# Cross-attention output projection as seven block products, and the first two up slices in one loop

## The chip, the core and the metric

The program runs on one core of a Trainium2 chip. The core has five engines with an instruction queue each: TensorE (PE, with PEld for its weight loads), VectorE (DVE), ScalarE (ACT), GpSimd (POOL) and SyncE (SP). The metric is the device time of one execution in microseconds (us). Before the change the median of three runs is 857.94 us (857.85 to 858.04). The profile is one more execution, of 858.13 us.

## The reference

One layer of an encoder on 512 tokens of width 1024, in float32: a token mixer with recurrent heads, a cross-attention to 256 memory tokens, and a squared-ReLU MLP, each added to the residual stream x, and a norm at the end. What matters here:

```python
def cross_attention(xn, memn, w_q, w_kv, w_o):
    q = (xn @ w_q).reshape(b, s, XATTN_HEADS, XATTN_HEAD_DIM)      # 4 heads of 256
    k, v = jnp.split(memn @ w_kv, 2, axis=-1)
    ...
    p = jax.nn.softmax(scores, axis=-1).astype(v.dtype)
    o = jnp.einsum('bhqk,bkhd->bqhd', p, v).reshape(b, s, D_MODEL)
    return o @ w_o                                                 # 512x1024 @ 1024x1024

x = x + cross_attention(rmsnorm(x, norm_xattn), rmsnorm(mem, norm_mem), w_q, w_kv, w_o)
x = x + jnp.square(jax.nn.relu(rmsnorm(x, norm_mlp) @ w_up)) @ w_down
```

## The kernel before, in words

**Number format.** Every projection is done in three passes of TensorE: an operand is split into a high part (a rounded copy, ACT, L232) and a low part (the rest, DVE, L233), and high x high, high x low and low x high are accumulated in one PSUM bank (`mm3`, L236 to L238). A weight block of 128x1024 is loaded by SP into one of three `st` buffers (L211) and split into one of three `wh`/`wl` pairs.

**Cross-attention.** The loop over the four heads (L904) projects q with `proj_d`, and puts a chain (`xattn_chain`) in a list. `tick()` takes the next step of the oldest chains, so that a head's scores, transposes and product with v (PV) are issued among the matmuls of the projection that follows. A head's output is os_[2h] and os_[2h+1], both transposed (features on the partitions, 512 tokens along them).

**Output projection.** `proj_res("xo", ...)` (L914) computes x + o @ w_o in eight pieces of 128 tokens by 512 columns (`xr[t, c]`, tiles named `vv`). For each column half c it takes four weight blocks of 256 rows, one for each head, and accumulates 4 token tiles x 8 feature tiles x 3 passes = 96 matmuls of 128x512; both halves take 192. The argument `drain` finishes all chains ahead of the fourth head's block. A finished piece is added to the residual (L823), its squares are summed (`stats`, ACT, L817), and `transp` turns it on TensorE (L831) and writes the high and low part of the MLP's input, `x3T[c]`, with four ACT and four DVE instructions (L836, L837). x3T[0] holds features 0 to 511, x3T[1] the rest.

**MLP.** The 4096 hidden features go in four blocks f. Each has eight up slices (`proj_d`, 24 matmuls each), and then the down projection of the block, which is already done in seven products instead of eight, in the manner of Strassen and Winograd (P1 to P7, L1048 to L1095). Tokens, features and columns are halved; the products take sums of weight blocks, "T2", "U" and "T3". POOL makes these sums by DMA: it loads a block into an `as` buffer (two of 128x2560) or a `gate` buffer (two of 128x1024), waits until it has landed, and issues the next block as an accumulating DMA on top (`sum_loads`, `add_block`, L937 to L952). The number g (0 or 1) is the half of a block's features that one weight tile holds. For f = 0 the sums are issued ahead of the first up slice.

**Order.** Up to the MLP a scheduler sets the order of the instructions on each engine; then TensorE keeps the order of the code (L1006). Each engine takes its instructions strictly in that order.

Of the kernel before, what the change touches and what calls it, by code (L numbers as in the profile page):

```python
# [11 lines left out]
F32R = mybir.dt.float32r  # L12
# [33 lines left out]
def _split_order():  # L46
    def d(m, c0, n):
        return [("d", m, 0, c0 + P * i) for i in range(n)]

    def t(m, k0, c0, n=4):  # L50
        return [("t", m, k0 + 2 * i, c0) for i in range(n)]

    seq = t("in", 0, 1536) + [("d", "gate", 0, 0)]
    for g in (0, 512, 1024, 2048):
        seq += d("in", g, 2)
    for g in (0, 512, 1024):
        seq += d("in", g + 256, 2)
# [12 lines left out]
    seq += [("t", "down", 8 * f + 2 * g, 512) for f in range(4) for g in range(2)]  # L70
    return seq


SEQ = _split_order()
SIDX = {key: i for i, key in enumerate(SEQ)}
NSTREAM = len(SEQ) - 8


@with_exitstack
def trunk(ctx: ExitStack, tc: tile.TileContext, x, mem, wpk, vec, cst, lmask, rmask, rows, out):  # L80
# [21 lines left out]
    def tiny(w):  # L102
        return sb.tile([P, w], F32, tag=f"tiny{w}", name=nm("tiny"), bufs=2 if w == 8 else 6)
# [809 lines left out]
    x3T = XT()
    proj_res("xo", 0, os_, (x3T, V_MLP), st2, drain)  # L914
    x3 = xk(x3T)
    ms2 = rstd_tok(st2)
    r4 = tiny(4)
    gp.tensor_tensor(out=r4, in0=ms2, in1=nh.to_broadcast([P, 4]), op=ALU.pow)
    rrow = RG()

    def rms_row():
        ps = smb()
        for t in range(4):
            pe.transpose(ps[:, t * P:t * P + P], r4[:, t:t + 1].to_broadcast([P, P]), ident)
        sc.activation(rrow[:, 0:512], ps, AF.Copy)

    ORDER = ("P1", "P2", "P6", "P5", "P7", "P3", "P4")  # L930
    JOBS = [("P1", 0), ("P2", 0), ("P1", 1), ("P2", 1)] + [(p, g) for p in ORDER[2:] for g in range(2)]
    jobs_hl, sums = {}, {}

    def block(f, g, kh, c):
        return SIDX["t", "down", 8 * f + 2 * g + 4 * kh, 512 * c]

    def sum_loads(f, names):  # L937

        parts = {"T2": ((0, 1), (1, 1), (0, 0)), "U": ((0, 1), (0, 0)), "T3": ((0, 1), (1, 1))}
        for nme in names:  # L940
            t = A16() if nme != "T3" else None
            for g in range(2):
                sums[f, nme, g] = G4()[:, :] if t is None else t[:, g * 1024:g * 1024 + 1024]
        for i in range(3):
            for nme in names:
                for g in range(2):
                    if i < len(parts[nme]):
                        add_block(sums[f, nme, g], block(f, g, *parts[nme][i]), i > 0)
# [40 lines left out]
    def add_to(t, c, ps, sign, fin=False):  # L989
# [13 lines left out]
        gp.tensor_tensor(out=r, in0=s1, in1=nh, op=ALU.pow)  # L1003
        finish(t, r, pieces[t])

    ctx.enter_context(tc.manual_schedule(engines={mybir.EngineType.PE}))  # L1006
    for f in range(4):

        sta = []
        sum_loads(f, ("T2", "U", "T3") if f == 0 else ("T2",))  # L1010
        for p in range(4):
            a = []
            for j in range(2):
                ps, = proj_d("up", 1024 * f + P * (p + 4 * j), x3, count=1)
                if f == 0 and p == 0 and j == 0:
                    rms_row()
# [31 lines left out]
        X, Y, Z = [smb(), smb()], [mmb(), mmb()], [smb(), smb()]  # L1048
        bank = {"P1": X, "P2": Y, "P5": Z, "P6": X, "P3": Z, "P7": X, "P4": X}
        into = {"P1": (0, 0, 1), "P2": (0, 0, 1), "P5": (2, 1, 1), "P6": (0, 1, -1), "P3": (0, 1, 1), "P7": (2, 1, -1), "P4": (2, 0, 1)}  # L1050
        last = {"P2", "P3", "P7", "P4"}

        def product(p, g, u, w, first, end):
            for k in range(2):
                ah, al = [t[:, u * P:u * P + P] for t in sta[2 * g + k][p]]
                bh, bl = [t[:, k * 512:k * 512 + 512] for t in w]
                new = first and k == 0 and p in ("P1", "P2", "P5")
                fl = dict(skip_group_check=True)
                ps = bank[p][u]
                pe.matmul(ps, lhsT=ah, rhs=bh, start=new, stop=False, **fl)  # L1060
                pe.matmul(ps, lhsT=ah, rhs=bl, start=False, stop=False, **fl)  # L1061
                pe.matmul(ps, lhsT=al, rhs=bh, start=False, stop=end and k == 1, **fl)  # L1062

        def ahead(n):
            with tc.high_priority():
                for m in range(n, n + 3):
                    job(f, m)
                i = max(hl_tiles)
                for m in range(i + 1, i + 4):
                    load(m)  # L1070
            if n == 8 and f < 3:
                sum_loads(f + 1, ("U", "T3"))
            return job(f, n)

        def done(p, u):
            t0, c, sign = into[p]
            add_to(t0 + u, c, bank[p][u], sign, fin and p in last)

        n = 0
        while n < len(JOBS):  # L1080
            p, g = JOBS[n]
            if p == "P4":
                ws = [ahead(n), ahead(n + 1)]
                for u in range(2):
                    for g in range(2):
                        product(p, g, u, ws[g], False, g == 1)
                    done(p, u)
                n += 2
                continue
            w = ahead(n)  # L1090
            for u in range(2):
                product(p, g, u, w, g == 0, g == 1)
                if g == 1:
                    done(p, u)
            n += 1  # L1095


# [88 lines left out]
```

## Time and profile before

| | |
|---|---|
| median of three runs | 857.94 us |
| profiled execution, its span | 858.13 us, 856.4 us |
| PE busy | 839.4 us, 98% of the span |
| DVE busy | 567.2 us, 66% |
| ACT busy | 423.9 us, 50% |
| POOL busy | 67.6 us, 8% |
| bytes moved | 113.62 MB, mean 133 GB/s |
| granted TensorE clock | 0.997 of full speed |

The span runs from the first to the last recorded instruction; the execution's own time is 1.7 us longer. A matmul row has its start and a length that includes the draining of the array; since matmuls overlap, what one costs is the distance between the starts of two. Of a wait, the row names the instruction that was waited for. The attention's fourth head and the output projection lie between 455 and 520 us.

### The profile page before, as it was taken

What the parts mean: (1) busy time and instruction counts of PE and PEld (TensorE: products, weight loads), DVE (VectorE), ACT (ScalarE), POOL (GpSimd) and SP (SyncE); (2) the same over time, 40 slices, a digit from 0 to 9 for tenths busy, and PEclk for the clock granted to TensorE, in tenths of its full rate; (3) what the DMA queues carried; (4) which work ended last, traced back from release to release, by engine and by line L of the source; (5) the groups of instructions that cost most, each with busy time, mean ns of one, the idle gap of its engine ahead of it and who ended that gap; (6) DMA issues with size and microseconds to landing.
All of it is one profiled execution on the core that took longest, in us unless ns stands there. A gap on an engine that the chain in (4) does not pass through costs nothing.

```text
span 856.4 us, 11676 instructions
## 1 busy us (share of the span) xinstructions
PE 839.4 (98%) x4438; PEld 692.3 (81%) x4438; DVE 567.2 (66%) x996; ACT 423.9 (50%) x773; POOL 67.6 (8%) x114
## 2 busy tenths in 40 slices
PE   7999999999999999999999999999999999999995
PEld 5888788887977987887888887888888888888884
DVE  5558875599368977555555446677567656756675
ACT  5336454444578485454444346453454344434544
POOL 2000000100010000100001200003101210220001
PEclk9999999999999999999999999999999999999998
DMA  7332224122142332532214842359935982698322
GB/s 266 128 116 77 72 77 137 41 99 81 71 127 74 110 130 91 183 104 98 75 50 130 201 136 96 92 127 237 276 108 143 275 246 99 179 288 196 123 51 98
DMA packets 32682, 113.62 MB, mean 133 GB/s; under 512 B 3761, under 2 KB 3889, under 8 KB 32626
## 3 DMA queue, kind: packets, MB, share of 16 engines
q1 hardware_dynamic: 23120, 78.84, 26.8%
q0 software_dynamic: 9216, 33.56, 17.7%
q8 instruction: 35, 0.57, 0.3%
q10 hardware_dynamic: 290, 0.47, 0.2%
q14 instruction: 21, 0.17, 0.1%
HBM read 110.76 MB, written 2.10 MB: 132 GB/s over the span
## 4 chain that ended last, share of the span: by engine, by line
PE 89%; issue 5%; DVE 2%; ACT 1%; DMA 1%; POOL 1%; POOLq 0%; SPq 0%; ACTq 0%; DVEq 0%
PE mm L236 20%; PE mm L237 20%; PE mm L238 19%; PE sm L1060 5%; PE sm L1061 5%; PE sm L1062 5%; PE sm L384 2%; PE sm L688 2%; PE sm L673 2%; PE sm L454 2%; PE mm L1061 1%; PE mm L1062 1%; PE mm L1060 1%; PE sm L238 1%; PE sm L237 1%
## 5 line engine op out<-in xcount | busy, mean ns | idle before, releaser
L232 ACT ACTIVATE wh<-st 128x1024 fp32r<-128x1024 f32 x133 | 141.0, 1060 | 216.3 <-PE mm L237 114.5
L233 DVE TENSOR_TENSOR wl<-st,wh 128x1024 fp32r<-128x1024 f32 x133 | 162.8, 1224 | 107.1 <-ACT wh L232 106.2
L236 PE MATMUL mm<-xT,wh 128*128 128x512 f32 x544 | 215.9, 398 | 0.0
L237 PE MATMUL mm<-xT,wh 128*128 128x512 f32 x544 | 213.3, 392 | 0.3 <-DVE xT L837 0.3
L238 PE MATMUL mm<-xT,wl 128*128 128x512 f32 x544 | 212.6, 391 | 0.0
L237 PEld LDWEIGHTS mm<-xT,wh 128*128 128x128 f32 x544 | 102.2, 188 | 22.9 <-DVE xT L837 2.0
L236 PEld LDWEIGHTS mm<-xT,wh 128*128 128x128 f32 x544 | 102.2, 188 | 21.9 <-issue 0.7
L238 PEld LDWEIGHTS mm<-xT,wl 128*128 128x128 f32 x544 | 102.1, 188 | 21.3 <-issue 0.2
L952 POOL DMA_DIRECT2D as<-in_wpk x48 | 36.7, 773 | 311.2 <-DVE wl L233 186.6
L1018 DVE SCALAR_TENSOR_TENSOR t<-mm,rg 128x512 f32<-128x512 f32 x32 | 22.1, 692 | 55.2 <-PE mm L238 55.0
L236 PE MATMUL mm<-wh,yT 128*128 128x512 f32 x128 | 50.6, 395 | 0.1
L238 PE MATMUL mm<-wh,yT 128*128 128x512 f32 x128 | 50.4, 394 | 0.0
L237 PE MATMUL mm<-wl,yT 128*128 128x512 f32 x128 | 50.3, 393 | 0.0
L1060 PE MATMUL sm<-wh,yT 128*128 128x512 f32 x128 | 49.8, 389 | 0.0
L1061 PE MATMUL sm<-wl,yT 128*128 128x512 f32 x128 | 49.8, 389 | 0.0
L1062 PE MATMUL sm<-wh,yT 128*128 128x512 f32 x128 | 49.8, 389 | 0.0
L232 ACT ACTIVATE wh<-as 128x1024 fp32r<-128x1024 f32 x24 | 25.5, 1062 | 33.3 <-PE sm L1062 23.7
L233 DVE TENSOR_TENSOR wl<-as,wh 128x1024 fp32r<-128x1024 f32 x24 | 29.4, 1226 | 13.6 <-ACT wh L232 13.6
L174 POOL TENSOR_TENSOR tiny<-tiny,misc 128x4 f32<-128x4 f32 (+1 forms) x14 | 12.0, 855 | 281.1 <-DVE tiny L172 281.0
L991 DVE TENSOR_TENSOR vv<-vv,sm 128x512 f32<-128x512 f32 x48 | 31.0, 681 | 1.2 <-PE sm L1062 1.2
L236 PEld LDWEIGHTS mm<-wh,yT 128*128 128x128 f32 x128 | 24.0, 188 | 5.3 <-DVE a L233 0.5
L232 ACT ACTIVATE yT<-t 128x512 fp32r<-128x512 f32 x32 | 19.8, 629 | 17.0 <-DVE t L1035 16.5
(275 smaller groups left out, 1509.2 us busy)
## 6 DMA issues: line engine op xcount, KB each, us to landing
st<-in_wpk SPq DMA_DIRECT2D x133, 512.0 KB, 3.3
as<-in_wpk POOLq DMA_DIRECT2D x48, 512.0 KB, 6.8
gate<-in_wpk POOLq DMA_DIRECT2D x16, 512.0 KB, 7.8
as<-in_x SPq DMA_DIRECT2D x4, 512.0 KB, 6.4
vv<-in_x SPq DMA_DIRECT2D x8, 256.0 KB, 4.1
out<-vv SPq DMA_DIRECT2D x7, 256.0 KB, 2.3
a<-in_mem SPq DMA_DIRECT2D x2, 512.0 KB, 5.5
t<-in_rows SPq DMA_DIRECT2D x2, 256.0 KB, 5.9
```

Source lines behind the costliest of these rows:

```text
L232: sc.activation(dst_hi, src, AF.Copy)
L233: v.tensor_tensor(out=dst_lo, in0=src, in1=dst_hi.bitcast(F32), op=ALU.subtract)
L236: pe.matmul(ps, lhsT=ah, rhs=bh, start=first, stop=False)
L237: pe.matmul(ps, lhsT=ah, rhs=bl, start=False, stop=False)
L238: pe.matmul(ps, lhsT=al, rhs=bh, start=False, stop=last)
L384: mm = pe.matmul(ps[64 * i:64 * i + 64, z:z + 64], lhsT=kc[j][:, w * P + 64 * i:w * P + 64 * i + 64], rhs=rhs(j, w * P, i), start=True, st ...
L952: gp.dma_start(out=dst, in_=wpk[idx], **kw)
L991: v.tensor_tensor(out=z, in0=z, in1=ps, op=ALU.add if sign > 0 else ALU.subtract)
L1018: v.scalar_tensor_tensor(out=y, in0=ps, scalar=0.0, in1=rrow[:, 0:512], op0=ALU.max, op1=ALU.mult)
L1060: pe.matmul(ps, lhsT=ah, rhs=bh, start=new, stop=False, **fl)
L1061: pe.matmul(ps, lhsT=ah, rhs=bl, start=False, stop=False, **fl)
L1062: pe.matmul(ps, lhsT=al, rhs=bh, start=False, stop=end and k == 1, **fl)
```

## The change

The output projection is computed as the down projection already was, by seven products of halves (f = -1 in the same code, now the function `by_blocks`). P1 takes the first token half of heads 0 and 1, P7 the difference of their two token halves, P2 and P4 the heads 2 and 3, and P3, P5 and P6 sums of all four heads. Their order is P1, P7, P2, P6, P5, P3, P4, each with g = 0 and 1 (g = 0: heads 0 and 2, g = 1: heads 1 and 3). P6 and P7 are each added to two column or token halves of the residual. POOL loads the sums T3 and T2 of w_o while the heads are projected, and U when the fourth head is drained, into the buffers that f = 0 had; f = 0's loads are put behind the instruction that makes the MLP's norm (`r4_made`). The attention chains make the sums of the heads' outputs and split them. `first_two` computes the first two up slices in one loop, first with the features 512 to 1023, then with 0 to 511.

The core of the diff:

```diff
-    seq += t("xo", 0, 0) + t("xo", 0, 512)
+    seq += t("xo", 0, 0) + t("xo", 4, 512, 2)
...
@@ xattn_chain
             split_out(d[:, 0:512], d[:, 512:1024], ps)
             os_[2 * h + j] = hl(d)
+            if j == 0:
+                one[h] = A4(F32R)
+            y1, z1 = one[h][:, j * 512:j * 512 + 256], one[h][:, j * 512 + 256:j * 512 + 512]
+            sa = T2()[:, 0:512]
+            if h < 2:
+                if j == 0:
+                    of[h] = A4()
+                o = of[h][:, j * 512:j * 512 + 512]
+                sc.activation(o, ps, AF.Copy)
+                v.tensor_tensor(out=sa[:, 0:256], in0=o[:, 0:256], in1=o[:, 256:512], op=ALU.subtract)
+                split_out(y1, z1, sa[:, 0:256])
+                sta_o[2 * h + j]["P7"] = (y1, z1)
+                continue
...
+            v.tensor_tensor(out=sa[:, 0:256], in0=x2_, in1=ps[:, 256:512], op=ALU.subtract)
+            v.tensor_tensor(out=sa[:, 256:512], in0=sa[:, 0:256], in1=x1, op=ALU.subtract)
+            v.tensor_tensor(out=s4, in0=ps[:, 0:256], in1=sa[:, 256:512], op=ALU.add)
+            split_out(ya[:, 0:512], ya[:, 512:1024], sa)
+            split_out(y1, z1, s4)
...
+    JOBS[-1] = [(p, g) for p in ("P1", "P7", "P2", "P6", "P5", "P3", "P4") for g in range(2)]
...
+    INTO[-1] = {**INTO[0], "P6": [(0, 1, -1), (2, 1, -1)], "P7": [(2, 1, -1), (2, 0, 1)]}
...
     for h in range(4):
+        if h > 1:
+            sum_loads(-1, (("T3",), ("T2",))[h - 2])
         qd[h] = []
...
-    proj_res("xo", 0, os_, (x3T, V_MLP), st2, drain)
...
+    def heads_in(p, g):
+        while p == "P7" and len(sta_o[2 * g + 1]) < 2:
+            tick()
+        while p == "P2" and len(sta_o[2 * g + 1]) < 7:
+            tick()
+        if (p, g) == ("P6", 0):
+            drain()
+            sum_loads(-1, ("U",))
+
+    def add_out(t, c, ps, sign, last):
+        z = xr[t, c]
+        v.tensor_tensor(out=z, in0=z, in1=ps, op=ALU.add if sign > 0 else ALU.subtract)
+        if last:
+            stats(st2, t, c)
+            whole.append((t, c))
+
+    def turn_whole():
+        while whole:
+            transp((x3T, V_MLP), *whole.pop(0))
...
+    by_blocks(-1, sta_o, (mm2, mm2, sm2, sm2), add_out, heads_in, turn_whole)
...
+    def first_two():
+        w = [weights(("d", "up", 0, P * 4 * j)) for j in range(2)]
+        two = [mmb(), mmb()]
+        for half in (4, 0):
+            for j in range(2):
+                for k in range(half, half + 4):
+                    z = slice(k * P, k * P + P)
+                    mm3(two[j], w[j][0][:, z], w[j][1][:, z], x3[k][0], x3[k][1], k == 4, k == 3)
+        rms_row()
+        return two
...
+        o = sum_loads(f, ("T2", "U", "T3") if f == 0 else ("T2",))
+        if f == 0:
+            for a in o:
+                behind(a, r4_made)
```

Three places show how the order moves; line numbers of the changed kernel differ (its L1014 to L1016 are the passes of a product, L1086 the add to the residual, L837 the turning, L843 the low part of x3T, L239 the low part of a split).

On DVE, the softmax of the fourth head stands before the change in this order (sm_4221 and sm_4222 are the scores of its two token halves):

```order
L871 TENSOR_REDUCE tiny_4247<-sm_4221 128x2
L872 TENSOR_TENSOR tiny_4247<-tiny_4247,misc 128x2
L871 TENSOR_REDUCE tiny_4247<-sm_4222 128x2
L878 RECIPROCAL tiny_4249<-tiny_4248 128x2
L872 TENSOR_TENSOR tiny_4247<-tiny_4247,misc 128x2
L881 TENSOR_SCALAR t_683_4252<-t_683_4252,tiny_4249 128x256 x2
```

After the change, two adds of P1's result (mm_4257 and mm_4258, one for each token tile) stand among them:

```order
L877 TENSOR_REDUCE tiny_4299<-sm_4274 128x2
L878 TENSOR_TENSOR tiny_4299<-tiny_4299,misc 128x2
L1086 TENSOR_TENSOR vv_3266<-vv_3266,mm_4257 128x512
L878 TENSOR_TENSOR tiny_4299<-tiny_4299,misc 128x2
L1086 TENSOR_TENSOR vv_3268<-vv_3268,mm_4258 128x512
L884 RECIPROCAL tiny_4301<-tiny_4300 128x2
L887 TENSOR_SCALAR t_700_4304<-t_700_4304,tiny_4301 128x256 x2
```

The second add has moved ahead of the reciprocal, whose result the probabilities and their transposes need.

On PE, the first two finished pieces of the residual (vv_3266 and vv_3268) are turned before the change among the last matmuls of the first column half:

```order
L236 MATMUL mm_4201<-wh_4293,yT_4318 128x512
L237 MATMUL mm_4201<-wl_4294,yT_4318 128x512
L831 MATMUL sm_4388<-cs,vv_3266 128x128 x4
L238 MATMUL mm_4201<-wh_4293,yT_4318 128x512
L831 MATMUL sm_4410<-cs,vv_3268 128x128 x4
L236 MATMUL mm_4201<-wh_4293,yT_4328 128x512
```

After it, they are turned within P6, in its second weight tile (wh_4457):

```order
L1014 MATMUL mm_4257<-wh_4457,xT_4256 128x512
L1015 MATMUL mm_4257<-wl_4458,xT_4256 128x512
L1016 MATMUL mm_4257<-wh_4457,xT_4256 128x512
L837 MATMUL sm_4477<-cs,vv_3266 128x128 x4
L1014 MATMUL mm_4257<-wh_4457,xT_4256 128x512
L837 MATMUL sm_4508<-cs,vv_3268 128x128 x4
```

The matmuls of P6 behind the turning, and all of P5, P3 and P4, now stand behind the two adds that complete these pieces.

On DVE, those two adds stood before the change behind the low parts of two streamed weight blocks (st):

```order
L233 TENSOR_TENSOR wl_4344<-st_4297,wh_4343 128x1024
L233 TENSOR_TENSOR wl_4374<-st_4347,wh_4373 128x1024
L823 TENSOR_TENSOR vv_3266<-mm_4199,vv_3266 128x512
L823 TENSOR_TENSOR vv_3268<-mm_4200,vv_3268 128x512
L837 SCALAR_TENSOR_TENSOR xT_4197<-sm_4388,vc,xT_4197 128x128
```

After it, they stand behind the low part of the sum U for g = 0 (as_4493 is the buffer of U), and the one for g = 1 follows them:

```order
L1086 TENSOR_TENSOR vv_3272<-vv_3272,sm_4358 128x512
L239 TENSOR_TENSOR wl_4499<-as_4493,wh_4498 128x1024
L1086 TENSOR_TENSOR vv_3266<-vv_3266,mm_4438 128x512
L1086 TENSOR_TENSOR vv_3268<-vv_3268,mm_4439 128x512
L239 TENSOR_TENSOR wl_4528<-as_4493,wh_4527 128x1024
L843 SCALAR_TENSOR_TENSOR xT_4255<-sm_4477,vc,xT_4255 128x128
L1086 TENSOR_TENSOR vv_3358<-vv_3358,mm_4257 128x512
L843 SCALAR_TENSOR_TENSOR xT_4255<-sm_4477,vc,xT_4255 128x128
```

U's splits now stand between TensorE's products and the adds, on ACT in the same way.

## Rows read from the trace of the kernel before

**Rows 1.** The page: busy time and share, then the chain that ended last.
```profile
PE 839.4 (98%) x4438; PEld 692.3 (81%) x4438; DVE 567.2 (66%) x996; ACT 423.9 (50%) x773; POOL 67.6 (8%) x114
...
PE 89%; issue 5%; DVE 2%; ACT 1%; DMA 1%; POOL 1%; POOLq 0%; SPq 0%; ACTq 0%; DVEq 0%
```

**Rows 2.** The waits of PE over the whole span: us, times, longest.
```profile
PE mm L237 <- DVE xT L837: 0.3, 1, 0.3
```

**Rows 3.** The timeline of PE: start us, us, engine, line, operation.
```profile
464.18 0.39 PE L236 MATMUL mm<-wh,yT 128*128 128x512 f32 x1
...
466.67 0.39 PE L238 MATMUL mm<-wh,yT 128*128 128x512 f32 x1
...
478.70 0.39 PE L238 MATMUL sm<-as,a 128*128 128x512 f32 x1
...
490.26 0.66 PE L831 MATMUL sm<-cs,vv 128*128 128x128 f32 x4
490.68 0.48 PE L238 MATMUL mm<-wh,yT 128*128 128x512 f32 x1
...
519.63 0.39 PE L236 MATMUL mm<-xT,wh 128*128 128x512 f32 x1
...
524.42 0.60 PE L924 MATMUL sm<-cs,tiny 128*128 128x128 f32 x4
```

**Rows 4.** The timeline of ACT: a weight split, a square, an evacuation of x3T.
```profile
472.72 1.06 ACT L232 ACTIVATE wh<-st 128x1024 fp32r<-128x1024 f32 x1 [0.45 <-PE mm L238]
...
514.02 0.63 ACT L817 ACTIVATE t<-vv 128x512 f32<-128x512 f32 x1 [1.89 <-DVE vv L823]
...
515.27 0.61 ACT L836 ACTIVATE xT<-sm,vc 128x128 fp32r<-128x128 f32 x2
```

**Rows 5.** The timeline of DVE: reciprocal, scale, weight split, add, x3T.
```profile
472.31 0.17 DVE L878 RECIPROCAL tiny<-tiny 128x2 f32<-128x2 f32 x1 [0.73 <-ACT t L876]
472.50 0.62 DVE L881 TENSOR_SCALAR t<-t,tiny 128x256 f32<-128x256 f32 x2
...
512.16 1.23 DVE L233 TENSOR_TENSOR wl<-st,wh 128x1024 fp32r<-128x1024 f32 x1 [4.22 <-ACT wh L232]
513.31 1.28 DVE L823 TENSOR_TENSOR vv<-mm,vv 128x512 f32<-128x512 f32 x2
...
520.25 1.12 DVE L837 SCALAR_TENSOR_TENSOR xT<-sm,vc,xT 128x128 fp32r<-128x128 f32 x4
```

**Rows 6.** The timeline of POOL when f = 0's sum U is loaded.
```profile
479.39 2.04 POOL L952 DMA_DIRECT2D as<-in_wpk  x3 [10.87 <-PE sm L238]
483.12 0.87 POOL L952 DMA_DIRECT2D as<-in_wpk  x1 [1.69 <-DMA as<-in_wpk]
```

**Rows 7.** POOL's accumulating DMAs in four short stretches: first and last start, landing.
```profile
L952 POOL DMA_DIRECT2D as<-in_wpk x2: 871/880/888, 465.8 to 467.7; - x2
...
DMA to landing us min/median/max: 7.2/7.5/7.9
...
L952 POOL DMA_DIRECT2D as<-in_wpk x2: 866/868/870, 483.1 to 485.8; - x2
...
DMA to landing us min/median/max: 9.0/9.9/10.9
...
L952 POOL DMA_DIRECT2D as<-in_wpk x2: 850/860/871, 604.8 to 606.1; - x2
...
DMA to landing us min/median/max: 6.6/7.6/8.5
...
L952 POOL DMA_DIRECT2D as<-in_wpk x1: 857/857/857, 652.9 to 652.9; - x1
...
DMA to landing us min/median/max: 5.2/5.2/5.2
```

**Rows 8.** Stretches: busy us of PE, PEld, DVE, ACT, POOL; clock; DMA share; GB/s.
```profile
6.00:9.00 3.00, 0.00 (x0) 0.00 (x0) 2.22 (x5) 2.21 (x3) 0.56 (x1) 1.00 1.02 414
...
850.00:851.00 1.00, 0.00 (x0) 0.00 (x0) 0.71 (x1) 0.71 (x1) 0.26 (x1) 0.93 0.13 47
```

More of the change, by code (lines that the diff above doesn't have):

```diff
@@ L168, in trunk, with behind @@
     negb = misc[:, 2:10]
+    def behind(a, b):
+        tc.add_manual_dep(a.ins, b.ins.name, mybir.DependencyInfo(mybir.DependencyClass.NoSync, mybir.DependencyReason.DATA),
+                          reason="order of an engine")
     def rstd_of(ss, w, n):
@@ new lines, in xattn_chain @@
+            p = 2 * (h - 2) + j
+            e = sta_o[p]
+            x1, x2_ = [of[h - 2][:, j * 512 + u:j * 512 + u + 256] for u in (0, 256)]
+            ya = A4(F32R)[:, :] if h == 2 else x3T[1][:, j * 1024:j * 1024 + 1024]
+            s4 = T2()[:, 0:256]
+            v.tensor_tensor(out=sa[:, 0:256], in0=x2_, in1=ps[:, 256:512], op=ALU.subtract)
+            v.tensor_tensor(out=sa[:, 256:512], in0=sa[:, 0:256], in1=x1, op=ALU.subtract)
+            v.tensor_tensor(out=s4, in0=ps[:, 0:256], in1=sa[:, 256:512], op=ALU.add)
@@ L930, in trunk @@
+            split_out(ya[:, 0:512], ya[:, 512:1024], sa)
+            split_out(y1, z1, s4)
+            e["P5"], e["P6"] = [(ya[:, u:u + 256], ya[:, 512 + u:768 + u]) for u in (0, 256)]
+            e["P3"] = (y1, z1)
+            for u, nme in enumerate(("P2", "P4")):
+                e[nme] = (d[:, u * 256:u * 256 + 256], d[:, 512 + u * 256:768 + u * 256])
+    of, one = {}, {}
+    sta_o = [{} for _ in range(4)]
     ORDER = ("P1", "P2", "P6", "P5", "P7", "P3", "P4")
-    JOBS = [("P1", 0), ("P2", 0), ("P1", 1), ("P2", 1)] + [(p, g) for p in ORDER[2:] for g in range(2)]
+    LATE = [(p, g) for p in ORDER[2:] for g in range(2)]
@@ L932, in trunk @@
+    JOBS = {f: [("P1", 0), ("P2", 0), ("P1", 1), ("P2", 1)] + LATE for f in range(4)}
+    JOBS[-1] = [(p, g) for p in ("P1", "P7", "P2", "P6", "P5", "P3", "P4") for g in range(2)]
     jobs_hl, sums = {}, {}
     def block(f, g, kh, c):
-        return SIDX["t", "down", 8 * f + 2 * g + 4 * kh, 512 * c]
+        return SIDX["t", "down" if f >= 0 else "xo", max(f, 0) * 8 + 2 * g + 4 * kh, 512 * c]
     def sum_loads(f, names):
@@ L940, in sum_loads @@
         for nme in names:
-            t = A16() if nme != "T3" else None
-            for g in range(2):
[L943 to L948, printed above, removed]
+            if nme == "T3":
+                t2 = [G4()[:, :] for _ in range(2)]
+            else:
+                t = A16()
+                t2 = [t[:, g * 1024:g * 1024 + 1024] for g in range(2)]
+            for g in range(2):
+                sums[f, nme, g] = t2[g]
+        return [add_block(sums[f, nme, g], block(f, g, *parts[nme][i]), i > 0)
+                for i in range(3) for nme in names for g in range(2) if i < len(parts[nme])]
     def add_block(dst, idx, accumulate=True):
         kw = dict(accum_op=ALU.add) if accumulate else {}
-        gp.dma_start(out=dst, in_=wpk[idx], **kw)
+        return gp.dma_start(out=dst, in_=wpk[idx], **kw)
     PLAIN = {"P1": (0, 0), "P2": (1, 0), "P3": (1, 1)}
@@ L975, in job, with by_blocks, product, ahead @@
         return jobs_hl[f, n]
+    INTO = {"P1": [(0, 0, 1)], "P2": [(0, 0, 1)], "P5": [(2, 1, 1)], "P6": [(0, 1, -1)], "P3": [(0, 1, 1)], "P7": [(2, 1, -1)],
+            "P4": [(2, 0, 1)]}
+    INTO = {f: INTO for f in range(4)}
+    INTO[-1] = {**INTO[0], "P6": [(0, 1, -1), (2, 1, -1)], "P7": [(2, 1, -1), (2, 0, 1)]}
+    LAST = {f: {"P2", "P3", "P4", "P7" if f >= 0 else "P5"} for f in JOBS}
+    def by_blocks(f, sta, banks, done, ready=None, after=None):
+        user = {"P1": 0, "P2": 1, "P5": 2, "P6": 0, "P3": 2, "P7": 0 if f >= 0 else 3, "P4": 0}
+        opens = {"P1", "P2", "P5"} if f >= 0 else {"P1", "P2", "P5", "P7"}
+        held = {}
+        def product(p, g, u, w, first, end):
+            for k in range(2):
+                ah, al = [t[:, u * P:u * P + P] for t in sta[2 * g + k][p]]
+                bh, bl = [t[:, k * 512:k * 512 + 512] for t in w]
+                new = first and k == 0 and p in opens
+                fl = dict(skip_group_check=True)
+                ps = held[user[p]][u]
+                pe.matmul(ps, lhsT=ah, rhs=bh, start=new, stop=False, **fl)
+                pe.matmul(ps, lhsT=ah, rhs=bl, start=False, stop=False, **fl)
+                pe.matmul(ps, lhsT=al, rhs=bh, start=False, stop=end and k == 1, **fl)
+            if after is not None:
+                after()
+        def ahead(n):
+            with tc.high_priority():
+                for m in range(n, n + 3):
+                    job(f, m)
+                i = max(hl_tiles)
+                for m in range(i + 1, i + 4):
+                    load(m)
+            if n == 8 and 0 <= f < 3:
+                sum_loads(f + 1, ("U", "T3"))
+            return job(f, n)
+        def finished(p, u):
+            for t0, c, sign in INTO[f][p]:
+                done(t0 + u, c, held[user[p]][u], sign, p in LAST[f] and (f >= 0 or len(INTO[f][p]) == 1))
+        n = 0
+        while n < len(JOBS[f]):
+            p, g = JOBS[f][n]
+            if ready is not None:
+                ready(p, g)
+            if user[p] not in held:
+                held[user[p]] = banks[user[p]]()
+            if p == "P4":
+                ws = [ahead(n), ahead(n + 1)]
+                for u in range(2):
+                    for g in range(2):
+                        product(p, g, u, ws[g], False, g == 1)
+                    finished(p, u)
+                n += 2
+                continue
+            w = ahead(n)
+            for u in range(2):
+                product(p, g, u, w, g == 0, g == 1)
+                if g == 1:
+                    finished(p, u)
+                elif ready is not None:
+                    tick()
+            n += 1
@@ new lines, in trunk @@
+    sm2, mm2 = (lambda: [smb(), smb()]), (lambda: [mmb(), mmb()])
+    for h in range(4):
+        if h > 1:
+            sum_loads(-1, (("T3",), ("T2",))[h - 2])
+        qd[h] = []
+        for ps in proj_d("xq", 256 * h, x2):
+            d = YT1()
+            split_out(d[:, 0:512], d[:, 512:1024], ps)
+            qd[h].append(d)
+        chains.append(xattn_chain(h))
+    st2 = misc[:, 34:42]
+    x3T = XT()
+    def heads_in(p, g):
+        while p == "P7" and len(sta_o[2 * g + 1]) < 2:
+            tick()
+        while p == "P2" and len(sta_o[2 * g + 1]) < 7:
+            tick()
+        if (p, g) == ("P6", 0):
+            drain()
+            sum_loads(-1, ("U",))
@@ new lines, in add_out @@
+    def add_out(t, c, ps, sign, last):
[4 more added lines that the diff above has]
+            whole.append((t, c))
+    whole = []
+    def turn_whole():
+        while whole:
+            transp((x3T, V_MLP), *whole.pop(0))
+    for p in range(4):
+        sta_o[p]["P1"] = tuple(t[:, 0:256] for t in os_[p])
+    by_blocks(-1, sta_o, (mm2, mm2, sm2, sm2), add_out, heads_in, turn_whole)
@@ L977, in finish, with rms_row @@
+    turn_whole()
+    drain()
+    x3 = xk(x3T)
+    ms2 = rstd_tok(st2)
+    r4 = tiny(4)
+    r4_made = gp.tensor_tensor(out=r4, in0=ms2, in1=nh.to_broadcast([P, 4]), op=ALU.pow)
+    rrow = RG()
+    def rms_row():
+        ps = smb()
+        for t in range(4):
+            pe.transpose(ps[:, t * P:t * P + P], r4[:, t:t + 1].to_broadcast([P, P]), ident)
+        sc.activation(rrow[:, 0:512], ps, AF.Copy)
     def finish(t, r, first):
@@ L1047, in trunk @@
             nc.sync.dma_start(out=gfin, in_=rows[3:4, :].to_broadcast([P, D]))
[L1048 to L1095, printed above, removed]
+        by_blocks(f, sta, (sm2, mm2, sm2), lambda t, c, ps, sign, last: add_to(t, c, ps, sign, fin and last))
 def _consts():
```

37 lines of the change are left out of this document (10 added, 27 removed).

## Prediction

> **What bounds the kernel now.** I read the page first. TensorE is busy 98% of the span, and 89% of the chain that ended last is PE [rows 1], so a matmul less is a matmul's time less, as long as nothing else makes PE wait. Then I read PE's waits: behind the attention only one is named, 0.3 us for the low part of the MLP's input at the first up slice [rows 2]. Next is PE's timeline: the first twelve matmuls of the output projection start between 464.18 and 466.67, eleven distances of 0.227 us [rows 3]. A row's 0.39 us is no cost, since the next one starts before it ends. Last come the queues that are to take over: ACT and DVE [rows 4, 5], and POOL with its accumulating DMAs [rows 6, 7]. They have slack on average; the question is what stands in front of what.
>
> My sum is made against the profiled execution's own 858.13 us (span 856.4 and 1.73 around it). That is 0.19 above the median of 857.94, so the forecast is set 0.2 lower at the end.
>
> **Part 1: fewer matmuls.** Eight pieces with 24 matmuls each, 192, become seven products with 24 each, 168. The number of turnings stays. 24 x 0.227 = 5.45 us less on PE, which is all on the path: **-5.45**.
>
> **Part 2: the first two up slices.** Before, the 18 matmuls from 519.63 to 524.42 take 4.79 us [rows 3], where 18 x 0.227 is 4.09. So the wait for x3T costs 0.7, more than the 0.3 that the waits name [rows 2], because several matmuls wait a little each. After, the first twelve matmuls read features 512 to 1023. Their last pieces are turned 18 matmuls and one turning ahead, 18 x 0.227 + 0.42 (the turning from 490.26 to 490.68 [rows 3]) = 4.5 us. In that time ACT has eight evacuations at 0.31 (half of 0.61), three squares at 0.63 and a split at some 1.0 [rows 4], together 5.4. I put the wait at 1.0: **+0.3** against before. Two up slices behind it leave the other half 5.4 us of cover, so the token half that comes last is no longer late.
>
> **Part 3: P1's add within the softmax of the fourth head.** In the new order of DVE the add of P1's second token tile stands ahead of the reciprocal. PE does P1's last matmul, and what stands next in its queue are the fourth head's transposes, which need the scaled probabilities. From that matmul's start: 0.39 until it ends [rows 3], 0.68 for an add (two take 1.28, and the second starts 0.60 behind the first), 0.19 from the reciprocal to the scale, 0.35 for the first half of the scale [rows 5], together 1.6. PE is ready 0.227 after the start, so it waits **+1.4**. Before, this add came much later, and the transposes at 472.52 waited for nothing. If the softmax's own steps ran slower than before, it would be some tenths more; it can't be under 1, because these four steps follow each other.
>
> **Part 4: the sum U in front of two adds.** This is the term that decides. U's buffer is that of the fourth head's probabilities, so its first loads are issued when PV ends. Before, f = 0's U had the same rule: the last PV matmul starts at 478.70 and ends at 479.09 [rows 3], POOL's first load starts at 479.39, 0.30 later, and the first accumulating one, which waits for a landing, at 483.12 [rows 6]. That is 3.73 for a plain load. Nothing on PE waited for it then, since U was used a whole MLP stage later. After, ACT and DVE have U's split in their queues ahead of the adds that complete vv_3266 and vv_3268, and PE has the turning of vv_3266 inside P6, ahead of U's own first matmul by 9 matmuls.
>
> From the start of the last PV matmul, PE does that one, 12 of P7, 24 of P2, 12 and 3 of P6: 52 x 0.227 = 11.8 us. In the same time: 0.39 + 0.30 + 3.73, then the landing of the accumulating load, then 1.06 for the high part [rows 4], 1.23 for the low part and 0.60 for the add [rows 5]. Without the landing this is 7.3, so PE waits for landing minus 4.5. The landing isn't shown for this place. The rows around are 7.2 and 9.0 for the first of a pair at 465.8 and 483.1, 6.6 at 604.8, 5.2 for a single one at 652.9 [rows 7]. At 483.1 a third sum was ahead of it; in the new kernel T2 has landed long before, and SP has few loads there because its buffers wait for the same queues. I take 6.6, the pair with the least beside it; the ends are 5.2 and 9.0. The wait is 6.6 + 7.3 - 11.8 = **+2.1** (0.7 to 4.5).
>
> The Trainium skill (DMA: Bandwidth & Descriptors, Anatomy of one DMA) puts a DMA of GpSimd at 2.0 us and its bytes over 436 GB/s, an estimate of 3.2 us for these 512 KB. By that the accumulating load would be early, part 4 would be nothing, and the sum 2.1 lower. The trace agrees for plain loads (3.73 with the issue of the next) but not for accumulating ones (5.2 at the least), so the rows hold.
>
> **Part 5: U for g = 1.** The second accumulating load lands 3.2 us behind the first (604.8 + 6.6 = 611.4 and 606.1 + 8.5 = 614.6 [rows 7]). Its split stands on DVE ahead of the turned pieces, of P6's four adds and of P5's first add, which the next turning needs. From its landing: 1.06 + 1.23 for the split, seven low parts of x3T at 0.28, four adds at 0.60, two weight splits at 1.15, and the add of 0.68 [rows 4, 5], together 9.3. So the piece is whole 12.5 us after the first landing. PE starts again 2.9 after the first landing (1.06 + 1.23 + 0.60), then has two turnings at 0.42, 9 matmuls of P6 and 24 of P5, 8.3 us: 11.2. It waits 1.3, and some tenths where ACT and DVE take turns on x3T: **+1.5** (0.7 if the landings are 2.4 apart, as 465.8 + 7.2 and 467.7 + 7.9 are; 2.9 if 4.7, as 483.1 + 9.0 and 485.8 + 10.9).
>
> **What costs nothing.** The head chains get 22 more ACT and 44 more DVE instructions here, beside PE's projections, where ACT is busy 50% and DVE 66% [rows 1]; without that cover each would cost its 0.4 to 0.7. POOL issues 16 more DMAs of 0.6 to 0.9, idle 92% of the time [rows 1]; SP issues two loads less. f = 0's sums now start behind r4_made, some 50 us ahead of the first product that uses them (eight slices at 5.45, and four tiles of P1 and P2 at 2.7), and three rounds need about 3.7 + 2 x 9. T2's second use in P4 is issued behind U's, with P5 and P3 in between.
>
> **Sum.** -5.45 + 0.3 + 1.4 + 2.1 + 1.5 = -0.15. 858.13 - 0.15 = 858.0, and on the median's scale 857.8. What seven products save is given back to three waits.
>
> **Rivals.** *The sums land early (faster).* With landings of 5.2, 2.4 apart, parts 4 and 5 are 0.7 each: -5.45 + 0.3 + 1.4 + 0.7 + 0.7 = -2.35, 855.6. For it: the single load at 652.9, and little other traffic. Against it: the two loads are a pair. If U were no wait at all, it would be -3.75, 854.2.
>
> *The sums land late (slower).* With 9.0, and 4.7 apart, as f = 0's U landed before, parts 4 and 5 are 4.5 and 2.9: -5.45 + 0.3 + 1.4 + 4.5 + 2.9 = +3.65, 861.6. Each us of the first landing is a us of the time, so it decides from a landing of about 8.5. For it: it is the same sum in the same place of the program. Against it: T2's accumulating load no longer goes before it. PE was idle from 6 to 9 us, and the granted clock stayed 1.00; it fell at 850 to 851, after the last matmul [rows 8]. The Trainium skill (TensorE: Matmul & The Clock Gate, Why this matters for your kernels) warns that idle gaps of a few us return the clock to 1.2 GHz. By that a late sum would also slow the matmuls behind it; at waits of 2 us no row here shows it.
>
> *Only the matmuls count.* If the order of the queues mattered little, the time would be 858.13 - 5.45, 852.5 on the median's scale. Part 3 alone speaks against it, and I give it 0.03, within the chance of early landings below.
>
> **Chances and range.** The forecast case (between -1.7 and +1.7, that is within 0.2%, about what a measurement of this kernel tells from no change) has 0.37; earlier landings, with no wait at all among them, 0.30; later ones 0.33, a little more because every estimate of a wait leaves out small delays. The likeliest time is 857.8, and its own range 856.2 to 859.6. The range for 8 in 10 reaches from the case without a wait for U to that of the late sums: 854.2 to 861.6.
>
> **What would show it.** In the changed profile: 168 matmuls on the three lines of the product in this stage; a PE wait of about 1.4 on DVE's scale (L887); one of about 2 at the turning (L837) for the add L1086, with a DVE split of an `as` buffer just before it and the landing of POOL's load before that; another of about 1.5 nine us later; at the first up slice about 1.0. Wrong it would be if PE's wait at the turning is absent or over 4, if PE waits in the MLP for f = 0's sums, or if the heads' extra splits delay P2.

## The result, and the profile after

| | before | after |
|---|---|---|
| median, 10 runs each | 858.00 us (857.44 to 858.40) | 860.10 us (857.39 to 861.09) |
| profiled execution, its span | 858.13, 856.4 us | 860.88, 858.5 us |

The ratio is 1.0023 (95% interval 1.0014 to 1.0031): 2.0 us slower (1.2 to 2.7). The forecast was no change, 857.8. The time lies inside the range, but on the side that had 0.33. Of the ten executions one took 857.39, the others 859.53 to 861.09.

The page of the changed kernel stands beside [rows 1]: PE is busy 3.2 us less, yet the span is longer.

```profile
PE 836.2 (97%) x4414; PEld 689.4 (80%) x4414; DVE 590.2 (69%) x1040; ACT 437.3 (51%) x795; POOL 79.4 (9%) x130
```

PE's waits from 440 to 535 us (us in total, times, longest), where before only the last kind was named [rows 2]:

```profile
PE sm L837 <- DVE vv L1086: 4.1, 2, 3.5
PE sm L894 <- DVE t L887: 1.2, 1, 1.2
PE mm L243 <- DVE xT L843: 0.8, 1, 0.8
```

All that was forecast to wait does. What it costs is read from PE's timeline (start us, us, engine, line, operation, the idle time before it and what ended it), as for [rows 3]:

```profile
464.99 0.39 PE L1014 MATMUL mm<-wh,yT 128*128 128x512 f32 x1
...
473.12 0.39 PE L1016 MATMUL mm<-wh,yT 128*128 128x512 f32 x1
474.76 0.44 PE L894 MATMUL sm<-cs,t 128*128 128x128 f32 x2 [1.25 <-DVE t L887]
...
492.73 0.39 PE L1016 MATMUL mm<-wh,xT 128*128 128x512 f32 x1
496.65 1.04 PE L837 MATMUL sm<-cs,vv 128*128 128x128 f32 x4 [3.54 <-DVE vv L1086]
497.35 0.78 PE L1014 MATMUL mm<-wh,xT 128*128 128x512 f32 x1
497.92 1.05 PE L837 MATMUL sm<-cs,vv 128*128 128x128 f32 x4
...
506.50 0.39 PE L1016 MATMUL sm<-wh,xT 128*128 128x512 f32 x1
507.49 0.66 PE L837 MATMUL sm<-cs,vv 128*128 128x128 f32 x4 [0.60 <-DVE vv L1086]
...
522.82 0.39 PE L242 MATMUL mm<-xT,wh 128*128 128x512 f32 x1
523.98 0.50 PE L243 MATMUL mm<-xT,wh 128*128 128x512 f32 x1 [0.77 <-DVE xT L843]
...
533.23 0.60 PE L1112 MATMUL sm<-cs,tiny 128*128 128x128 f32 x4
533.58 0.48 PE L242 MATMUL mm<-xT,wh 128*128 128x512 f32 x1
```

A gap is the distance of two starts less the 0.227 us of a matmul. At the transposes it is 474.76 - 473.12 - 0.23 = 1.41, at the first turning 496.65 - 492.73 - 0.23 = 3.69, at the next 0.76, at the first up slice 0.93, with 0.1 in the rows behind it. The turning at 496.65 takes 1.04 us; in [rows 3] one takes 0.66. The stretches around it (us; busy us of PE, PEld, DVE, ACT, POOL; granted clock; DMA share; GB/s) show why:

```profile
490.00:492.50 2.50, 2.50 (x13) 2.06 (x11) 0.95 (x3) 0.00 (x0) 0.57 (x1) 1.00 0.93 174
496.00:497.00 1.00, 0.34 (x2) 0.35 (x3) 1.00 (x3) 0.82 (x1) 0.00 (x0) 0.89 1.04 205
497.00:498.00 1.00, 1.00 (x6) 0.82 (x5) 0.93 (x2) 1.00 (x4) 0.00 (x0) 0.50 1.03 205
...
499.00:500.00 1.00, 1.00 (x3) 0.76 (x3) 0.14 (x1) 0.62 (x2) 0.00 (x0) 0.50 0.53 107
500.00:501.00 1.00, 1.00 (x5) 0.81 (x4) 1.00 (x4) 0.15 (x1) 0.00 (x0) 0.90 0.09 16
501.00:502.00 1.00, 1.00 (x6) 0.79 (x6) 1.00 (x4) 0.68 (x2) 0.00 (x0) 1.00 0.00 0
```

PE stood still from 492.96 to 496.65, and the granted clock behind it is 0.50, the level of 1.2 GHz, until about 500.5. The eight rows from 496.65 to 500.36 exceed their full-speed distances (0.35 for four transposes, 0.227 for a matmul) by 0.35, 0.34, 0.36, 0.34, 0.20, 0.19, 0.08 and nothing: **1.86 us** that no wait names. PE reads as busy in these stretches, so its busy share hides the loss.

The sum over the stage runs from the first matmul of the projection to the first one behind `rms_row`. Before, that one is

```profile
524.78 0.48 PE L236 MATMUL mm<-xT,wh 128*128 128x512 f32 x1
```

so the stage takes 60.60 us from 464.18 [rows 3]; after, it takes 68.59 us, from 464.99 to 533.58. Both have 216 such matmuls of the projection and of up: 24 fewer of the projection, and 24 more of up, which the rest of the program is spared. So 68.59 - 60.60 - 5.45 = +2.54. The two profiled executions differ by 2.75. Besides these 2.54 there are 0.81 more ahead of the stage, 1.23 less from the last matmul to the span's end (it starts at 845.65 before and at 848.98 after), and 0.65 more outside the span; the cause of these three stays open.

Last, why it took so long: POOL's first accumulating load of U, as [rows 7] had its kind before.

```profile
L969 POOL DMA_DIRECT2D as<-in_wpk x1: 887/887/887, 485.6 to 485.6; - x1
...
DMA to landing us min/median/max: 8.0/8.0/8.0
```

```profile
493.69 1.06 ACT L238 ACTIVATE wh<-as 128x1024 fp32r<-128x1024 f32 x1 [4.72 <-DMA as<-in_wpk]
494.78 1.22 DVE L239 TENSOR_TENSOR wl<-as,wh 128x1024 fp32r<-128x1024 f32 x1 [3.83 <-ACT wh L238]
495.92 1.28 DVE L1086 TENSOR_TENSOR vv<-vv,mm 128x512 f32<-128x512 f32 x2
```

The first of these groups is POOL's row. The second follows the landing: ACT's high part of U had waited 4.72 us for it, DVE's low part waited for ACT, and behind it come the two adds, the first of which PE's turning waits for.

### The profile page after: what moved, and what is told of

Its sections match the earlier page's. It is cut to its first block, busy times and chain, and to the rows that moved or that the text cites. A ratio compares the mean times of both kernels' runs of the same rounds, so it can differ in the third digit from the quotient of the medians.

```text
span 858.5 us, 11724 instructions
## 1 busy us (share of the span) xinstructions
PE 836.2 (97%) x4414; PEld 689.4 (80%) x4414; DVE 590.2 (69%) x1040; ACT 437.3 (51%) x795; POOL 79.4 (9%) x130
## 4 chain that ended last, share of the span: by engine, by line
PE 86%; issue 5%; DVE 3%; DMA 3%; ACT 2%; POOL 1%; POOLq 0%; ACTq 0%; DVEq 0%
PE mm L242 18%; PE mm L243 18%; PE mm L244 18%; PE sm L1014 5%; PE sm L1015 5%; PE sm L1016 5%; PE sm L390 2%; PE sm L694 2%; PE sm L679 2%; PE sm L460 2%; DMA as<-in_wpk 1%; PE mm L1014 1%; PE mm L1015 1%; PE mm L1016 1%; DVE wl L239 1%
## 5 line engine op out<-in xcount | busy, mean ns | idle before, releaser
L238 ACT ACTIVATE wh<-st 128x1024 fp32r<-128x1024 f32 x131 | 138.9, 1061 | 197.0 <-PE mm L243 108.3
L239 DVE TENSOR_TENSOR wl<-st,wh 128x1024 fp32r<-128x1024 f32 x131 | 160.2, 1223 | 88.6 <-ACT wh L238 87.6
L969 POOL DMA_DIRECT2D as<-in_wpk x60 | 45.8, 772 | 297.8 <-DVE wl L239 163.7
L238 ACT ACTIVATE wh<-as 128x1024 fp32r<-128x1024 f32 x30 | 31.9, 1062 | 42.5 <-PE sm L1016 23.7
L1014 PE MATMUL sm<-wh,yT 128*128 128x512 f32 x128 | 49.8, 389 | 0.0
L1016 PE MATMUL sm<-wh,yT 128*128 128x512 f32 x128 | 49.8, 389 | 0.0
L239 DVE TENSOR_TENSOR wl<-as,wh 128x1024 fp32r<-128x1024 f32 x30 | 36.7, 1225 | 18.3 <-ACT wh L238 18.1
L1015 PE MATMUL sm<-wl,a 128*128 128x512 f32 x84 | 32.9, 391 | 0.0
L1014 PE MATMUL sm<-wh,a 128*128 128x512 f32 x84 | 32.9, 391 | 0.0
L1016 PE MATMUL sm<-wh,a 128*128 128x512 f32 x84 | 32.8, 390 | 0.0
L1014 PEld LDWEIGHTS sm<-wh,yT 128*128 128x128 f32 x128 | 24.0, 188 | 5.0
L1016 PEld LDWEIGHTS sm<-wh,yT 128*128 128x128 f32 x128 | 24.0, 188 | 5.0
```

Source lines behind the costliest of these rows:

```text
L969: return gp.dma_start(out=dst, in_=wpk[idx], **kw)
```

## Experiments

Theory from this profile: U's late landing costs 3.69 at the turning, and the idle PE loses its clock on top. Rivals: the order on DVE is at fault, whoever lands when; the slow rows have another cause; ACT and DVE are simply too full.

**1. Fill the gap with work (fill).**

```diff
+                if (f, p, g, u, k) == (-1, "P6", 1, 0, 0):
+                    junk = smb()
+                    for m in range(16):
+                        d = pe.matmul(junk, lhsT=ah, rhs=bh, start=True, stop=True)
...
+                    after()
+                    behind(turned[0], d)
```

The last two lines put both turnings right behind the sixteen matmuls; in the changed kernel one matmul of P6 stands between them.

> Sixteen matmuls of 128x512 into a bank that nobody reads are put on PE ahead of the turning of vv_3266, where the changed kernel's profile has a gap of 3.69 us: 16 x 0.227 = 3.63 us of work in place of idling. Theory (the gap also costs the clock): the granted clock stays at 1.00 behind it, the turning and the eight matmuls behind it run at full speed, and 1.86 us come back: 858.2. Rival (the slow matmuls behind the gap have another cause, such as ACT and DVE being behind): they stay long, and the time is the same or longer by what the sixteen exceed the gap, 860.0 to 860.5.

Measured: 858.2 us (857.75 to 860.13, 11 runs). Its PE has no gap at the turning:

```profile
492.23 3.79 PE L1024 MATMUL sm<-wh,xT 128*128 128x512 f32 x16
495.86 1.03 PE L839 MATMUL sm<-cs,vv 128*128 128x128 f32 x8
496.65 0.48 PE L1018 MATMUL mm<-wh,xT 128*128 128x512 f32 x1
```

and the stretch behind it runs at the full clock:

```profile
496.00:500.00 4.00, 4.00 (x24) 3.44 (x22) 3.50 (x9) 3.68 (x11) 0.00 (x0) 1.00 0.75 146
```

The turning starts 3.86 us behind the start of P6's third matmul, 3.92 in the changed kernel, and the next turning waits 1.21 in place of 0.76. So 1.9 us came back (860.1 to 858.2) though PE was held from its work as long. The 1.86 are the clock's, caused by the idling; ACT and DVE had the same work as in the changed kernel.

**2. The adds ahead of U's split (adds_first, adds_pinned).**

```diff
+            o = split_out(hi, lo, s_)
+            if (f, p, g) == (-1, "P5", 0):
+                behind(o[1], added["P2"])
```

Adds_pinned also holds P4's matmuls behind P3's.

> U's low part for g = 0 is put behind the two adds of P2's result on DVE; nothing else is asked for. My theory: the wait at the turning is a matter of what stands ahead of the adds in DVE's queue. The adds need only P2's matmuls, which end at about 490, so PE finds the pieces whole and turns them without a wait, the granted clock stays 1.00, and U is met at its own first matmul (P5, g = 0): in the changed kernel's profile its low part ends at 496.0 and PE would be there at 492.96 + 2 x 0.35 + 9 x 0.227 = 495.7, a wait of 0.3. That gives back 3.69 + 1.86 - 0.3 = 5.2 us: about 854.9. Rival: U's landing bounds the stage wherever it is waited for, so the wait only moves from the turning to P5 and the clock falls there: a gain of at most the 2.7 us of work that is passed, 857.4 to 860.

> As adds_first, and P4's matmuls are held behind P3's on PE, as the changed kernel has them; in adds_first six of them had moved ahead of P3 and waited for T2's split (gaps of 1.99, 1.27 and 0.91 us, the slow clock behind them). Theory: without that, the adds ahead of U's split give back the wait at the turning and the clock: a gap of some 0.4 at P5 remains, and the time is 855 to 856. Rival (ACT and DVE can't keep up behind a late U, so some product behind waits in any order): gaps of 2 us or more at P5 or P3, 858 to 860.

Measured: 861.06 (858.75 to 861.61) and 861.08 (859.60 to 862.53). The theory fell in both, and the rivals' times, 860 at most, were too low too. In adds_first the wait at P5 is small as expected (0.36), but P4's matmuls ahead of P3 wait 1.99, 1.27 and 0.91 us with one matmul between two waits, and the clock falls there as well:

```profile
508.00:510.00 2.00, 2.00 (x7) 1.61 (x6) 0.66 (x2) 1.23 (x4) 0.00 (x0) 0.50 0.00 0
```

In adds_pinned the first turning waits for nothing (it starts at 491.59), but the next one does, for 3.99 us. DVE shows what had happened:

```profile
490.64 1.28 DVE L1090 TENSOR_TENSOR vv<-vv,mm 128x512 f32<-128x512 f32 x2
493.20 1.23 DVE L239 TENSOR_TENSOR wl<-as,wh 128x1024 fp32r<-128x1024 f32 x1 [1.28 <-ACT wh L238]
...
503.23 1.23 DVE L239 TENSOR_TENSOR wl<-as,wh 128x1024 fp32r<-128x1024 f32 x1
504.37 1.29 DVE L1090 TENSOR_TENSOR vv<-vv,sm 128x512 f32<-128x512 f32 x2
```

The adds are done by 491.9, then DVE still waits for U. From then on it works through splits, low parts of x3T and P6's adds without a pause of over 0.6 us, and the add that the next turning needs is its last, at 504.37. The wait had only been passed on, and the clock fell again, 0.75 in the mean from 505 to 508:

```profile
505.00:508.00 3.00, 2.89 (x13) 2.39 (x14) 1.49 (x5) 2.32 (x7) 0.00 (x0) 0.75 0.00 0
```

**3. Less traffic beside U (t2_late).**

```diff
-            if p == "P6":
+            if p == "P6" and f >= 0:
                 add_block(s_, block(f, g, 1, 0))
...
+                o = gp.tensor_tensor(out=tiny(4), in0=sums[-1, "U", 0][:, 0:4], in1=nh.to_broadcast([P, 4]), op=ALU.mult)
+                for m in range(2):
+                    behind(add_block(sums[-1, "T2", m], block(-1, m, 1, 0)), o)
```

> The two accumulating loads of T2 for P4, which now start at 487.9 and 489.7 beside U's, are put behind U's landing for g = 0 on POOL (a tiny POOL operation that reads U stands ahead of them). Theory: U's accumulating loads share the DMA engines with T2's; alone, U for g = 0 lands some 6.6 us after its issue, not 8.0, and the wait at the turning falls from 3.7 to 2.3, with less of the clock's loss: about 858.2. Rival: an accumulating load of 512 KB takes its 8 us by itself: the landing stays at 7.5 to 8, and the time at 860.

Measured: in the profiled execution the landing is 6.9 us in place of 8.0, and the gap 2.85 in place of 3.69:

```profile
L969 POOL DMA_DIRECT2D as<-in_wpk x1: 893/893/893, 485.1 to 485.1; - x1
...
DMA to landing us min/median/max: 6.9/6.9/6.9
```

That T2's loads made the difference is not shown. No_two (experiment 7) has the changed kernel's orders up to the MLP, issues T2's loads at nearly the same times (the last at 489.5, there at 489.7), and its U landed sooner still:

```profile
L969 POOL DMA_DIRECT2D as<-in_wpk x1: 890/890/890, 485.6 to 485.6; - x1
...
DMA to landing us min/median/max: 6.4/6.4/6.4
```

In the other traces with T2's loads behind it the same load took 6.6 (adds_pinned), 7.3 (softmax), 7.5 (fill) and 8.4 us (adds_first). So the landing varies by 2 us from trace to trace, and the 6.9 lies within that.

The time shows no gain either: 857.33 in the profiled execution, whose clock stays 1.00 behind the gap (row below), and 860.61 to 861.31 in the five others, which left no trace. Over the whole span the mean granted clock is 0.996 in the first and 0.993 to 0.994 in the five, so they lost some clock; where is not shown.

```profile
495.00:500.00 5.00, 4.93 (x26) 4.24 (x27) 4.96 (x11) 4.50 (x12) 0.00 (x0) 1.00 0.99 192
```

**4. U early, all orders kept (u_gate).** T3 leaves its two `gate` buffers when it is split, 10 us and more before PV ends.

```diff
-            if nme == "T3":
+            if nme == "T3" or (f, nme) == (-1, "U"):
```

> U of the output projection goes into the two gate buffers, which are free once T3 is split at about 470, and not into the buffer of the fourth head's probabilities, which is free at 481.5. The order of the instructions on PE, DVE and ACT is that of the changed kernel. Theory (the late U costs the wait at the turning, the slow clock behind it and the next wait): the accumulating loads land before 485, the turning of vv_3266 waits for nothing, the granted clock is 1.00, and 3.69 + 1.86 + 0.76 = 6.3 us go: from 860.1 to 853.8. Rival (the wait at the turning comes from ACT and DVE being loaded with splits and x3T, whoever lands when): the pieces are still late at the turning by 1 to 2 us, and the time is 857 to 858.

Measured: 854.74 us (854.16 to 855.58), ratio to before 0.9957 (0.9944 to 0.9970). U's first loads start at 467.21 and 471.05, and PE turns at once:

```profile
492.41 0.40 PE L1016 MATMUL mm<-wh,xT 128*128 128x512 f32 x1
492.64 0.60 PE L837 MATMUL sm<-cs,vv 128*128 128x128 f32 x4
493.00 0.48 PE L1014 MATMUL mm<-wh,xT 128*128 128x512 f32 x1
493.31 0.60 PE L837 MATMUL sm<-cs,vv 128*128 128x128 f32 x4
```

This is 5.4 us better than the changed kernel, for 3.69 + 1.86 = 5.55 of U's wait and the clock. The rival, ACT and DVE too full whoever lands when, asked for 857 to 858. One line of the expectation was wrong: the gap of 0.76 at the second turning is still there, so it never was the late U's.

**5. U without its second block (u_plain).**

```diff
-        ... "U": ((0, 1), (0, 0)), ...
+        ... "U": ((0, 1), (0, 0))[:2 if f >= 0 else 1], ...
```

> As the changed kernel, and U of the output projection is one plain load; the accumulating load of its second block is left out, and with it that part of the sum. It shows what the accumulating load costs. Theory: the plain load lands 3.8 us after its issue at 481.9, before PE needs it; no wait at the turning, no slow clock: 860.1 - 3.69 - 1.86 = 854.6, as with U in the gate buffers. Rival (the splits on ACT and DVE alone make the pieces late): a wait of over 1 us at the turning stays, 857.

Measured: 854.71 us (854.52 to 855.50), gaps as in u_gate. The buffer of the fourth head's probabilities is early enough for a plain load, which lands in 3.5 to 4.2 us; the second load, which waits for the first and accumulates on top of it, is the whole loss.

**6. The add within the softmax (softmax).** P1's second add goes behind the scale.

```diff
+            behind(p1[1], scaled[3, 0])
```

> The second add of P1 is put behind the reciprocal and the scales of the fourth head's first two tiles on DVE. By the prediction's part 3 the add is what makes the transposes late: the wait of 1.41 at the transposes falls by an add's 0.6 to 1.2, 859.0 to 859.5. Rival, from the changed kernel's profile: the last sum of an exponential comes from ACT at 474.02 and the reciprocal starts at 474.16, so the softmax's own steps set the time and the add covers only 0.1: no change, 860.0.

Measured: the gap at the transposes is 1.30 in place of 1.41. DVE now waits for ACT's sum of exponentials where the add had stood:

```profile
472.37 0.15 DVE L878 TENSOR_TENSOR tiny<-tiny,misc 128x2 f32<-128x2 f32 x1
473.19 0.17 DVE L884 RECIPROCAL tiny<-tiny 128x2 f32<-128x2 f32 x1 [0.66 <-ACT t L882]
```

So the add cost 0.1; the rival holds. The time, 861.56 (861.02 to 863.38), is no evidence on it: six matmuls of P4 had moved ahead of P3 and waited there, gaps of 1.35 and 0.81, while U's wait stayed (3.54).

**7. The up slices one after the other (no_two).**

```diff
-            two = first_two() if f == p == 0 else None
+            two = None
```

> The first two up slices are computed one after the other again, features 0 to 511 first, as before the change; all else is the changed kernel's. The pieces of features 0 to 511 are the last to be whole, so the first up slice waits for the add, the turning and the evacuation of the last two: by rows 0.7 + 0.4 + 0.7, less what runs beside, some 2.0 to 2.5 in place of 0.9: 861.2 to 861.7. Rival (the first two slices together hide nothing here): 860.1.

Measured: 863.87 us (862.54 to 866.18), worse than expected. The last turning, now ahead of the first up slice, waits 4.08, the slice 0.93 more (it starts at 523.03, 1.28 behind the turning at 521.75, of which 0.35 is the turning's own), and the clock falls behind it:

```profile
523.00:526.00 3.00, 2.97 (x8) 2.40 (x9) 1.42 (x5) 1.10 (x3) 3.00 (x5) 0.58 0.27 61
```

Computing the two together is worth 3.8 us here (863.87 - 860.10), since the last two pieces have no cover else.

**8. Filling the softmax's gap as well (banks, best_pin).** On top of u_gate, P7's sums go to the `mm` banks and P2's to `sm`; in best_pin P4 is also held behind P3, and the transposes behind those six matmuls of P7.

```diff
-    by_blocks(-1, sta_o, (mm2, mm2, sm2, sm2), add_out, heads_in, turn_whole)
+    by_blocks(-1, sta_o, (mm2, sm2, sm2, mm2), add_out, heads_in, turn_whole)
```

> As u_gate, and P7's products go to the bank pair of P2 and P2's to P7's (mm for P7, sm for P2). On PE six matmuls of P7 then stand ahead of the transposes of the fourth head's probabilities. Theory: the wait of 1.41 at these transposes is the softmax's own time with nothing beside it, and six matmuls fill 6 x 0.227 = 1.36 us of it: from 854.7 to 853.4. Rival: the transposes, PV and P2 start later by those six matmuls, so the time comes back behind them: 854.7.

> As banks, with P4's matmuls held behind P3's on PE. Theory: of banks' order only two matmuls of P4, which stand ahead of the second turning and wait for T2's split, are moved; a gap of up to 0.5 us goes: 853.0 to 853.4. Rival: those two cover the add that the turning waits for, and without them the turning waits as in u_gate: 853.8.

Measured: 854.56 (854.03 to 855.19) and 854.46 (853.84 to 854.54). Six matmuls of P7 do fill the gap at the transposes (banks):

```profile
473.95 0.39 PE L1016 MATMUL mm<-wh,a 128*128 128x512 f32 x1
474.23 0.70 PE L894 MATMUL sm<-cs,t 128*128 128x128 f32 x4
```

But of the 1.41 most is given back: in best_pin the two turnings wait 0.63 and 1.08 (0 and 0.76 in u_gate). Best_pin beats both kernels, 0.9952 of before (0.9939 to 0.9964), 3.8 us less than its 858.24; that it beats u_gate lies within their spread.

## Why the prediction was wrong

| step | predicted | measured |
|---|---|---|
| part 1: 24 matmuls fewer | -5.45 | -5.47 from the stage's end to the last matmul |
| part 2: first up slices | +0.3 | +0.3 (0.93 + 0.1, before 0.7) |
| part 3: transposes | +1.4 | +1.41, for another reason |
| part 4: U ahead of two adds | +2.1 (0.7 to 4.5) | +3.69 |
| the clock behind that wait | 0 | +1.86 |
| part 5: U for g = 1 | +1.5 | +0.76, for another reason |
| sum | -0.15 | +2.6; the stage shows +2.54 |

Two terms failed, and both lie at one place.

**Part 4 was mis-sized.** The mechanism was right: its sum (landing + 7.3 - 11.8) gives 3.5 with the landing of 8.0, and 3.69 was measured. I had taken 6.6 for the landing, from a pair of loads in the MLP with little beside it. The slip was to put one value, near the low end, on a time that varies: in six traces with the same loads behind it, this load landed in 6.4 to 8.4 us. Why it varies stays open. T2's loads for P4 start some 2 to 4 us behind it (at 487.5 and 489.7), and the costs set at nothing had them only as "issued behind U's"; that they slow it is not shown (experiment 3).

**The clock was priced at nothing.** The case of a late sum named it, and then left it out "at waits of 2 us"; even its sum of +3.65, with a wait of 4.5, has no term for it. Here the clock was 0.50 behind a gap of 3.69 us, which cost 1.86, and experiment 1 shows that the idling is the cause. The Trainium skill (TensorE: Matmul & The Clock Gate, Why this matters for your kernels) has the rule that an idle gap of a few us costs the clock. This trace agrees. The gap's length alone does not decide it in these runs: the clock was 1.00 behind the 2.85 of t2_late's trace, and fell in adds_first, where the longest of three waits was 1.99.

The two feed on each other: in this execution 1.4 us more landing than assumed went with 1.6 us more wait and 1.86 of clock. With the landing of 6.6 the forecast's mechanism stands, as no_two's trace shows: 6.4, a gap of 2.40, and the clock at 1.00 behind it. The one execution at 857.39 may be such a case, but it left no trace.

**Part 3 was right in size by chance.** Not the add, but the softmax's own steps are late (experiment 6). DVE of the changed kernel, from its last weight split before them:

```profile
470.23 1.23 DVE L239 TENSOR_TENSOR wl<-gate,wh 128x1024 fp32r<-128x1024 f32 x1 [1.07 <-ACT wh L238]
471.37 1.28 DVE L877 TENSOR_REDUCE tiny<-sm 128x2 f32<-128x512 f32 x2
```

The softmax begins at 471.37, behind T3's split, and the transposes come 3.39 us later; PE is out of other matmuls at 473.35. Before, it began at 468.53, with no split in front of it:

```profile
468.53 0.69 DVE L871 TENSOR_REDUCE tiny<-sm 128x2 f32<-128x512 f32 x1 [1.46 <-PE sm L238]
```

The transposes at 472.52 were 3.99 behind that, and PE had work until then. That T3's split is what delays the softmax is read from the order of these rows; no run moved it.

**Part 5** put 1.5 on U for g = 1. The 0.76 that came stays with U early (u_gate), so it is DVE's queue alone. Why the wait for the second landing didn't add to it is argued, not shown: when the first wait is long, PE is late itself, and what comes behind U has caught up. Experiment 2 shows the other face: take the first wait away and the second becomes 3.99.

The steps that cost nothing did so: no wait of PE is named in the MLP for f = 0's sums, and P2 starts with no gap.

## What to carry to other kernels

When a wait on TensorE is a few us, price the matmuls behind it at the lower clock too, or put work in the gap. When an engine waits in order for a late transfer, moving what the wait hits only moves the wait; ask first which buffer lets the transfer start earlier (here one line, 5.4 us). A landing time from one trace is one draw: the same load took 6.4 to 8.4 us here, so carry such a term as a range, and price what its far end sets off.

## What the hardware showed

An accumulating load of 512 KB by GpSimd took 6.4 to 8.4 us to land in six traces with the same loads issued behind it; plain ones issued by GpSimd 4 us earlier took 3.5 to 4.5. Behind gaps of 3.69 (changed kernel), 3.54 (softmax) and 3.99 us (adds_pinned) matmuls ran at the lower clock for some 3 to 4 us, 1.6 to 1.9 us lost each; so did those behind three gaps of 1.99, 1.27 and 0.91 us in a row (adds_first). Behind single gaps of 2.85 (t2_late) and 2.40 (no_two) they ran at full speed.
